# A decoder-layer kernel on one Trainium2 core: two additions moved into accumulating DMAs, level masks left out, conv taps of one instruction each, and another load order in the FFN's second product

## The chip, the cores and the metric

The kernel runs on one core of a Trainium2 chip, in one launch. The metric is the device time of that launch in microseconds (us), lower is better. A core has five engines that run their own instruction streams in order and wait for each other by semaphores: PE (matmuls; its weight loads are counted as PEld), DVE, ACT, POOL and SP. DMAs are issued from the queues of SP and of POOL and move data by 16 shared DMA engines.

## What is computed

One step of a hybrid decoder layer on 1024 prompt tokens and 8 x 8 sample tokens, width 1024, all in float32. Cut to what matters here:

```python
def swiglu(x, w_in, w_out):
    gate, up = jnp.split(x @ w_in, 2, axis=-1)
    return (jax.nn.silu(gate) * up) @ w_out

x = x + 0.5 * swiglu(rmsnorm(x), w_ffn1_in, w_ffn1_out)          # D_FF = 2816
qkv_raw, z, a, b, q_s, k_s, v_s, gate_a, gate_b = split(rmsnorm(x) @ w_in)
ext = concat([conv_buf, qkv_raw])                                # 4 taps
q, k, v = split(silu(sum(conv_w[j] * ext[:, j:j + L] for j in range(4))))
# gated delta rule, 8 heads of 128:
decay = exp(where(incl, gc[..., :, None] - gc[..., None, :], -inf))
A = where(strict, (k * beta) @ k.T * decay, 0)
T = triangular_solve(A + eye, eye)
...
o_g = rmsnorm(o_g) * silu(z)
o_s = windowed attention with sinks (q_s, k_s, v_s)
mixed = sigmoid(gate_a) * o_g + sigmoid(gate_b) * o_s
x = x + mixed @ w_out
x = x + 0.5 * swiglu(rmsnorm(x), w_ffn2_in, w_ffn2_out)
y = rmsnorm(x)
```

## The kernel before

All matmuls are done on a float32 value split into a high and a low part (`split`, L225 on ACT casts the high part, L226 on DVE subtracts it to get the low part); a product is three matmuls (L250 to L252, in the second product of the FFN L713 to L715). 1088 columns of tokens (1024 and 64) lie beside each other; in the GDN they are nine chunks of 128.

The stages in order: the first FFN (its first product, then the second, `ffn_out`, from about 528 us), the attention, the GDN (`gdn`, about 1150 to 1950 us, in which the dense products of all heads are woven between the recurrences of others), the out projection and the second FFN (`ffn2`; its `ffn_out` starts at about 2525 us).

**FFN-out.** It works in seven products j with five groups of weight tiles each. `rights` (L602 on) loads the rows of h from DRAM (hq, hd) into two buffers h0 and h1 in turn, and splits each into x0 to x3. `lefts` loads the weights into w0, w1, tq (as w2 and v) and w3, in halves k = 0 and 1, splits them into u0 to u3, and has POOL and DVE form the sums of halves (L653 to L660). For j = 0 only the halves k = 0 are needed. Loads go out on SP's queue in the order in which they are written (`keep_in_program_order`); a load waits on the queue until its buffer is free, and holds what stands behind it. `rights` issues the load of step i + 2 behind the split of step i; `lefts` issues in j = 0, from the second group on, the next group's half 0 and the previous group's half 1.

**Conv taps** (`conv_taps`). The input ext holds 1024 prompt columns and then eight blocks of 11 sample columns. Four taps per q, k and v of a head: the first on ACT (L1205, L1206), three on DVE (L1208 on 1024 columns, L1209 on 8 x 8), then silu on ACT (L1210).

**Decay** (`decay`). SP loads a broadcast of the head's cumulated gates into dm (128 x 1152, 576 KB; L1330), ACT applies nine Relus (L1333, one per chunk) and an Exp (L1334), POOL multiplies by two masks (L1335, L1336). `stage_t` then uses dm on DVE (L1367, L1462).

**Levels** (`levels`). The triangular inverse is put together in two block levels from A (the tile am0). For each, POOL masks a part of A into `am` (L1410, L1437), PE multiplies it with the inverse so far (L1416, L1440), ACT copies the results out (x2z L1421, t4 L1433, x3z L1441), and PE multiplies again (L1426, L1445). Each head has three such groups of chunks.

**Gated output** (`gdn_out`). The attention has written its gated part to the DRAM tensor me. Behind each of three parts of a head's gated output zg, POOL loads me (L1652) and adds it (L1653), then stores zg to md (L1655). `ffn2` loads md into its tiles a.

The order on each engine comes from a planner at build time, which sees data dependencies and its own estimates; it is the same in each run. POOL's and SP's instructions and DMAs are executed in order too.

Of the kernel before, what the change touches and what calls it, by code (L numbers as in the profile page):

```python
# [18 lines left out]
P = 128  # L19
# [33 lines left out]
def constants():  # L53
# [17 lines left out]
        "m2": (j // 64 == i // 64) & (j % 64 < 32) & (i % 64 >= 32),  # L71
        "m3": (j < 64) & (i >= 64),
# [4 lines left out]
        "new": np.where(new, 0.0, NEG),  # L77
    }
# [77 lines left out]
class Core:  # L156
# [34 lines left out]
    def setup(self):  # L191
# [12 lines left out]
        self.md = self.dp.tile([H, P, T], F32, name="md")  # L204
# [402 lines left out]
    def rights(self):  # L607
# [11 lines left out]
        for i, (n, _) in enumerate(src):  # L619
            z = fo[f"h{i % 2}"].rearrange("p (n t) -> p n t", n=2)[:, :n]  # L620
            out = self.split_to(f"x{i % 4}", z, i < 2)
            load(i + 2)
            yield out

    def lefts(self, w_out):
# [13 lines left out]
        load(0, 0)  # L639
        for j in range(7):  # L640
            for i in range(len(GROUPS)):
                a11, a21, a12, a22 = quads(i)
                if j == 0 and i:
                    if i == 1:
                        load(1, 0)
                    load(i + 1, 0)
                    load(i - 1, 1)
                if j == 1 and i == 0:
                    load(len(GROUPS) - 1, 1)
# [544 lines left out]
    def conv_taps(self, h, d, u):  # L1194
        nc, v = self.nc, self.nc.vector
        self.lab = f"h{h}"
        blk, u_ = u * 8 + h, "qkv"[u]
        y, ext = d[u_], d["ext", u]
        es = ext[:, 1027:1115].rearrange("p (b j) -> p b j", j=11)
        v.memset(y[:, T:], 0.0)  # L1200
        ys = y[:, LP:T].rearrange("p (b t) -> p b t", t=NT)
        for j in range(4):
            wc = self.cw[:, j * 24 + blk:j * 24 + blk + 1]
            if j == 0:
                nc.scalar.mul(y[:, :LP], ext[:, 0:LP], wc)  # L1205
                nc.scalar.mul(ys, es[:, :, 0:NT], wc)  # L1206
            else:
                v.scalar_tensor_tensor(out=y[:, :LP], in0=ext[:, j:j + LP], scalar=wc, in1=y[:, :LP], op0=ALU.mult, op1=ALU.add)  # L1208
                v.scalar_tensor_tensor(out=ys, in0=es[:, :, j:j + NT], scalar=wc, in1=ys, op0=ALU.mult, op1=ALU.add)  # L1209
        nc.scalar.activation(y[:, :T], y[:, :T], AF.Silu)  # L1210
# [14 lines left out]
    def gdn(self):  # L1225
        nc, v = self.nc, self.nc.vector
        with ExitStack() as st:
            gp = self.pool("gdn", stack=st)
            a, n = self.off["m2"]
            self.m2 = gp.tile([P, 2, 32], F32, name="m2")  # L1230
            nc.sync.dma_start(self.m2, self.i["c_pack"][:, a:a + n].rearrange("p (b u j) -> p b u j", b=2, u=2)[:, :, 1, :])
            a, n = self.off["m3"]
            self.m3 = gp.tile([P, 64], F32, name="m3")
            nc.sync.dma_start(self.m3, self.i["c_pack"][:, a + 64:a + n])
# [12 lines left out]
            bp = Pools(self, st, ("L", "X", "pr", "am"), ("S0", "kg", "vt", "qk"), ("t4",), ("R", "o1", "vn", "S", "jk", "*"), ("ot", "zg", "me", "s4"), ("e",), ("y",), ("dm", "am0"))  # L1247
# [78 lines left out]
    def decay(self, bp, h, d):  # L1326
# [4 lines left out]
                          self.rw[h * NCH:(h + 1) * NCH, :].rearrange("(o c) t -> o (c t)", o=1).broadcast_to([P, TP]))  # L1331
        for c in range(NCH):
            nc.scalar.activation(dm[:, c], dm[:, c], AF.Relu, scale=-1.0, bias=self.gc[:, h, c:c + 1])  # L1333
        nc.scalar.activation(dm, dm, AF.Exp, scale=-1.0)  # L1334
        nc.gpsimd.tensor_tensor(out=dm[:, 0:8], in0=dm[:, 0:8], in1=self.tri[:, None, :].broadcast_to([P, 8, P]), op=ALU.mult)  # L1335
        nc.gpsimd.tensor_tensor(out=dm[:, 8], in0=dm[:, 8], in1=self.tris, op=ALU.mult)  # L1336
# [69 lines left out]
    def levels(self, bp, h, A, t4):  # L1406
        nc, v = self.nc, self.nc.vector
        self.lab = f"h{h}"
        am = bp.tile([P, 4, 2, 32], F32, tag="am", bufs=2, name=self.name("am"))
        nc.gpsimd.tensor_tensor(out=am, in0=A.rearrange("p c (b u j) -> p c b u j", b=2, u=2)[:, :, :, 1, :],  # L1410
                                in1=self.m2[:, None].broadcast_to([P, 4, 2, 32]), op=ALU.mult)
# [530 lines left out]
```

## Time and profile before

| | us |
|---|---|
| median of 3 runs (2808.99 to 2811.06) | 2810.89 |
| profiled execution | 2810.84 |
| its span | 2809.1 |
| PE busy | 2691.2 |
| DVE busy | 1982.4 |
| ACT busy | 1237.3 |
| POOL busy | 563.7 |

Mean granted clock of PE 0.983. The chain of work that ended last is PE in 77% of the span, DVE 9%, DMA 5%, ACT 3%, issue 3% and POOL 1%. The profile is of one execution; its time is that of the median run. "Waits" rows give an engine's idle time by the instruction that stood waiting and the one that released it; in a timeline the brackets hold the idle time just ahead of the instruction and its releaser. The granted clock is a share of full speed, 1.00 and 0.50 being the two levels of 2.4 and 1.2 GHz.

### The profile page before, as it was taken

The numbers are of one execution on the slowest core, as the hardware profiler recorded it, in microseconds if no ns is written. First come the engines' busy times: TensorE is split into PE (matmuls) and PEld (weight loads), VectorE is DVE, ScalarE is ACT, GpSimd is POOL, SyncE is SP. The second block draws the span as 40 slices with busy tenths as digits, with TensorE's granted clock in tenths as the row PEclk, the third lists the DMA queues.
The fourth block names the chain that finished last, engine by engine and source line by source line (L and its number), as shares of the span: only waits on it lengthen the run. The fifth ranks groups of instructions, "written<-read, shape, count | busy, mean of one in ns | idle before, by whom it ended". The sixth has DMA issues, their size and how long they took to land.

```text
span 2809.1 us, 50868 instructions
## 1 busy us (share of the span) xinstructions
PE 2691.2 (96%) x19887; PEld 2523.4 (90%) x19887; DVE 1982.4 (71%) x4502; ACT 1237.3 (44%) x2904; POOL 563.7 (20%) x585
## 2 busy tenths in 40 slices
PE   6999999999989999999999999999999999998998
PEld 6899999999978888887788888888989999997998
DVE  6777787564665777777887776785678878767545
ACT  5333322233334767753655455546444233223333
POOL 3222221231010000031332222221002212205110
PEclk9999999999999999999999999999999999999999
DMA  4243322546332333342333333334533322216562
GB/s 143 91 158 127 112 101 90 191 135 144 107 105 54 85 85 78 97 100 63 90 98 78 67 94 90 89 82 145 191 118 117 103 88 102 100 57 237 129 147 78
DMA packets 236871, 306.66 MB, mean 109 GB/s; under 512 B 14405, under 2 KB 184214, under 8 KB 236598
## 3 DMA queue, kind: packets, MB, share of 16 engines
q1 hardware_dynamic: 203252, 222.21, 25.9%
q0 software_dynamic: 33312, 81.19, 10.6%
q8 instruction: 156, 2.56, 0.4%
q14 instruction: 85, 0.70, 0.1%
q10 hardware_dynamic: 66, 0.02, 0.0%
HBM read 212.19 MB, written 84.19 MB: 106 GB/s over the span
## 4 chain that ended last, share of the span: by engine, by line
PE 77%; DVE 9%; DMA 5%; ACT 3%; issue 3%; POOL 1%; SPq 0%; DVEq 0%; ACTq 0%; POOLq 0%
PE pst L252 13%; PE pst L250 13%; PE pst L251 13%; PE pst L715 4%; PE pst L714 4%; PE pst L713 4%; PE psgh L250 3%; PE psgh L251 3%; PE psgh L252 3%; PE psg L250 3%; PE psg L252 3%; PE psg L251 3%; PE pso L943 1%; DMA adr<-am0h 1%; PE pst L936 1%
## 5 line engine op out<-in xcount | busy, mean ns | idle before, releaser
L251 PE MATMUL pst<-x,u 128*128 128x256 f32 (+3 forms) x2656 | 780.4, 294 | 1.0 <-DVE x L226 1.0
L250 PE MATMUL pst<-x,u 128*128 128x256 f32 (+3 forms) x2040 | 610.8, 300 | 12.1 <-ACT x L225 11.1
L252 PE MATMUL pst<-x,u 128*128 128x256 f32 (+3 forms) x2040 | 605.6, 297 | 0.0
L251 PEld LDWEIGHTS pst<-x,u 128*128 128x128 f32 x2656 | 503.8, 190 | 7.1 <-DVE x L226 1.5
L250 PEld LDWEIGHTS pst<-x,u 128*128 128x128 f32 x2040 | 386.3, 190 | 19.3 <-ACT x L225 12.6
L252 PEld LDWEIGHTS pst<-x,u 128*128 128x128 f32 x2040 | 387.4, 190 | 4.6
L225 ACT CAST u<-raw 128x512 fp32r<-128x512 f32 x308 | 186.4, 617 | 323.3 <-PE pst L252 300.6
L715 PE MATMUL pst<-x,u 128*128 128x272 f32 x1008 | 293.3, 292 | 13.8 <-DVE u L226 13.8
L252 PE MATMUL psgh<-xhl,wlh 128*128 128x512 f32 (+2 forms) x912 | 303.7, 333 | 0.0
L713 PE MATMUL pst<-x,u 128*128 128x272 f32 x1008 | 290.6, 292 | 7.4 <-ACT x L225 7.1
L714 PE MATMUL pst<-x,u 128*128 128x272 f32 x1008 | 293.2, 292 | 4.5 <-DVE x L226 4.5
L226 DVE TENSOR_TENSOR u<-raw,u 128x512 fp32r<-128x512 f32 x308 | 216.5, 712 | 49.6 <-ACT u L225 49.3
L334 DVE TENSOR_TENSOR tm<-pst,tm 128x256 f32<-128x256 f32 (+1 forms) x400 | 168.0, 434 | 103.0 <-PE pst L252 100.9
L252 PE MATMUL pst<-xhl,u 128*128 128x256 f32 (+2 forms) x808 | 237.8, 295 | 2.5 <-DVE u L226 2.5
L250 PE MATMUL pst<-xhl,u 128*128 128x256 f32 (+2 forms) x808 | 236.7, 294 | 2.2 <-ACT u L225 2.2
L715 PEld LDWEIGHTS pst<-x,u 128*128 128x128 f32 x1008 | 192.8, 191 | 14.6 <-DVE u L226 14.6
L713 PEld LDWEIGHTS pst<-x,u 128*128 128x128 f32 x1008 | 191.6, 192 | 8.3 <-ACT x L225 7.5
L714 PEld LDWEIGHTS pst<-x,u 128*128 128x128 f32 x1008 | 192.9, 191 | 4.9 <-DVE x L226 4.9
L252 PEld LDWEIGHTS psgh<-xhl,wlh 128*128 128x128 f32 x912 | 172.9, 190 | 12.2
L252 PEld LDWEIGHTS pst<-xhl,u 128*128 128x128 f32 x808 | 153.2, 190 | 5.9 <-DVE u L226 2.9
L250 PEld LDWEIGHTS pst<-xhl,u 128*128 128x128 f32 x808 | 152.8, 190 | 5.3 <-ACT u L225 2.4
L250 PE MATMUL psg<-xhl,whc 128*128 128x512 f32 (+2 forms) x456 | 153.3, 336 | 1.1 <-DVE ring L814 1.1
(686 smaller groups left out, 6356.3 us busy)
## 6 DMA issues: line engine op xcount, KB each, us to landing
raw<-in_w_ffn_in_dram SPq DMA_DIRECT2D x48, 1024.0 KB
h<-hq SPq DMA_DIRECT2D x56, 544.0 KB
hq<-sg POOLq DMA_DIRECT2D x45, 544.0 KB, 3.6
rawh<-in_w_in_dram SPq DMA_DIRECT2D x38, 512.0 KB
w<-in_w_ffn_out_dram SPq DMA_DIRECT2D x14, 1024.0 KB
raw<-in_w_in_dram SPq DMA_DIRECT2D x21, 512.0 KB
ring<-ring SPq DMA_DIRECT2D x32, 272.0 KB
t4h<-tdr POOLq DMA_DIRECT2D x32, 256.0 KB, 5.1
```

The costliest lines, as they stand in the source:

```text
L225: keep(self.nc.scalar.copy(hi, src))
L226: return keep(self.nc.vector.tensor_tensor(out=lo, in0=src, in1=hi.bitcast(F32), op=ALU.subtract))
L250: nc.tensor.matmul(out, w[0], x[0], start=start, stop=False)
L251: nc.tensor.matmul(out, w[0], x[1], start=False, stop=False)
L252: nc.tensor.matmul(out, w[1], x[0], start=False, stop=stop)
L334: v.tensor_tensor(out=out, in0=pb, in1=t[:, i, :n], op=ALU.add)
L713: nc.tensor.matmul(pb, w[0], y[0], start=first, stop=False, skip_group_check=True)
L714: nc.tensor.matmul(pb, w[0], y[1], start=False, stop=False, skip_group_check=True)
L715: nc.tensor.matmul(pb, w[1], y[0], start=False, stop=end, skip_group_check=True)
L936: nc.tensor.transpose(out=pt[:, kb, r], in_=sm[:, r, kb * P:(kb + 1) * P], identity=self.ident)
L943: nc.tensor.matmul(po, w[:, ks // P + kb].rearrange("p a b -> p (a b)"), x[:, kb].rearrange("p r q -> p (r q)"), start=i + kb == 0, stop=i ...
```

## The change

- `decay`: a constant `later` (0 where the mask was 1, NEG elsewhere, 128 x 1152) is added to dm by an accumulating DMA on POOL's queue, behind the broadcast and ahead of the Relus. The two mask multiplies are gone.
- `levels`: the masks m2 and m3, the tile `am` and the two mask multiplies of each group are gone; PE reads A itself.
- `conv_taps`: each tap is one instruction on 1112 columns that runs over the prompt and the sample blocks alike; silu is two instructions, and the memset stands behind it.
- `gdn_out`: zg is added to me in DRAM by one accumulating DMA; the loads of me, POOL's adds and the store to md are gone, and `ffn2` reads me.
- `rights`: the load of step i + 1 is issued ahead of the split of step i, from the second step on. `lefts`: a table says at which step which half is loaded; the halves k = 1 come a group later, and w1 and w2 ahead of the third h load.

```diff
--- before.py
+++ after.py
@@ -68,13 +68,12 @@
         "suf": j > i,
         "sufs": same8 & (j > i),
         "m1": (j // 32 == i // 32) & (j % 32 < 16) & (i % 32 >= 16),
-        "m2": (j // 64 == i // 64) & (j % 64 < 32) & (i % 64 >= 32),
-        "m3": (j < 64) & (i >= 64),
         "bm": (np.arange(P)[:, None] // 8 == np.arange(NB)[None, :]),
         "band": np.where(band, 0.0, NEG),
         "first": np.where(first, 0.0, NEG),
         "cache": np.where(cache, 0.0, NEG),
         "new": np.where(new, 0.0, NEG),
+        "later": np.concatenate([np.where(j <= i, 0.0, NEG)] * 8 + [np.where(same8 & (j <= i), 0.0, NEG)], axis=1),
     }
     off, parts, at = {}, [], 0
     for k, v in mats.items():
@@ -201,7 +200,6 @@
         self.hq = self.dp.tile([7, NS // 2, P, HT], F32, name="hq")
         self.xt = self.dp.tile([P, KD, T], F32, name="xt")
         self.xd = self.dp.tile([P, KD, T], F32, name="xd")
-        self.md = self.dp.tile([H, P, T], F32, name="md")
         self.me = self.dp.tile([H, P, T], F32, name="me")
         self.cols = self.cp.tile([P, 33], F32, name="cols")
 
@@ -617,10 +615,10 @@
         load(0)
         load(1)
         for i, (n, _) in enumerate(src):
+            if i:
+                load(i + 1)
             z = fo[f"h{i % 2}"].rearrange("p (n t) -> p n t", n=2)[:, :n]
-            out = self.split_to(f"x{i % 4}", z, i < 2)
-            load(i + 2)
-            yield out
+            yield self.split_to(f"x{i % 4}", z, i < 2)
 
     def lefts(self, w_out):
 
@@ -636,17 +634,12 @@
             return [ws[i][:, :, k, 512 * h:512 * h + 512] for k in range(2) for h in range(2)]
 
         at = 0
-        load(0, 0)
+        order = {(0, 0): ((0, 0),), (0, 1): ((1, 0), (2, 0)), (0, 2): ((3, 0), (0, 1)), (0, 3): ((4, 0), (1, 1)), (0, 4): ((2, 1), (3, 1)), (1, 0): ((4, 1),)}
         for j in range(7):
             for i in range(len(GROUPS)):
                 a11, a21, a12, a22 = quads(i)
-                if j == 0 and i:
-                    if i == 1:
-                        load(1, 0)
-                    load(i + 1, 0)
-                    load(i - 1, 1)
-                if j == 1 and i == 0:
-                    load(len(GROUPS) - 1, 1)
+                for z in order.get((j, i), ()):
+                    load(*z)
                 if j == 2:
                     n = GROUPS[i][1]
                     s = fo[f"S{i % 2}"].rearrange("p (n c) -> p n c", c=512)[:, :n]
@@ -1196,18 +1189,16 @@
         self.lab = f"h{h}"
         blk, u_ = u * 8 + h, "qkv"[u]
         y, ext = d[u_], d["ext", u]
-        es = ext[:, 1027:1115].rearrange("p (b j) -> p b j", j=11)
-        v.memset(y[:, T:], 0.0)
-        ys = y[:, LP:T].rearrange("p (b t) -> p b t", t=NT)
+        n = 1112
         for j in range(4):
             wc = self.cw[:, j * 24 + blk:j * 24 + blk + 1]
             if j == 0:
-                nc.scalar.mul(y[:, :LP], ext[:, 0:LP], wc)
-                nc.scalar.mul(ys, es[:, :, 0:NT], wc)
+                nc.scalar.mul(y[:, :n], ext[:, 0:n], wc)
             else:
-                v.scalar_tensor_tensor(out=y[:, :LP], in0=ext[:, j:j + LP], scalar=wc, in1=y[:, :LP], op0=ALU.mult, op1=ALU.add)
-                v.scalar_tensor_tensor(out=ys, in0=es[:, :, j:j + NT], scalar=wc, in1=ys, op0=ALU.mult, op1=ALU.add)
-        nc.scalar.activation(y[:, :T], y[:, :T], AF.Silu)
+                v.scalar_tensor_tensor(out=y[:, :n], in0=ext[:, j:j + n], scalar=wc, in1=y[:, :n], op0=ALU.mult, op1=ALU.add)
+        nc.scalar.activation(y[:, :LP], y[:, :LP], AF.Silu)
+        nc.scalar.activation(y[:, LP:T].rearrange("p (b t) -> p b t", t=NT), y[:, 1027:1115].rearrange("p (b j) -> p b j", j=11)[:, :, :NT], AF.Silu)
+        v.memset(y[:, T:], 0.0)
 
     def tail_out(self, bp, h, tails):
         nc = self.nc
@@ -1226,12 +1217,6 @@
         nc, v = self.nc, self.nc.vector
         with ExitStack() as st:
             gp = self.pool("gdn", stack=st)
-            a, n = self.off["m2"]
-            self.m2 = gp.tile([P, 2, 32], F32, name="m2")
-            nc.sync.dma_start(self.m2, self.i["c_pack"][:, a:a + n].rearrange("p (b u j) -> p b u j", b=2, u=2)[:, :, 1, :])
-            a, n = self.off["m3"]
-            self.m3 = gp.tile([P, 64], F32, name="m3")
-            nc.sync.dma_start(self.m3, self.i["c_pack"][:, a + 64:a + n])
             self.gn = self.cols[:, 32:33]
             self.x2z = gp.tile([P, 4, 2, 32], F32, name="x2z")
             self.x3z = gp.tile([P, 4, 64], F32, name="x3z")
@@ -1244,7 +1229,7 @@
             for u in range(2):
                 for z in range(2):
                     nc.gpsimd.dma_start(self.rows_view(self.td[u], z), self.rsm[:, None, :].broadcast_to([P, NCH, P]))
-            bp = Pools(self, st, ("L", "X", "pr", "am"), ("S0", "kg", "vt", "qk"), ("t4",), ("R", "o1", "vn", "S", "jk", "*"), ("ot", "zg", "me", "s4"), ("e",), ("y",), ("dm", "am0"))
+            bp = Pools(self, st, ("L", "X", "pr"), ("S0", "kg", "vt", "qk"), ("t4",), ("R", "o1", "vn", "S", "jk", "*"), ("ot", "zg", "s4"), ("e",), ("y",), ("dm", "am0"))
             hd = [dict() for _ in range(H)]
             wv = Weave(self)
 
@@ -1329,11 +1314,11 @@
         dm = d["dm"] = bp.tile([P, NCH, P], F32, tag="dm", bufs=2, name=self.name("dm"))
         nc.sync.dma_start(dm.rearrange("p c t -> p (c t)"),
                           self.rw[h * NCH:(h + 1) * NCH, :].rearrange("(o c) t -> o (c t)", o=1).broadcast_to([P, TP]))
+        a, n = self.off["later"]
+        nc.gpsimd.dma_start(dm.rearrange("p c t -> p (c t)"), self.i["c_pack"][:, a:a + n], accum_op=ALU.add)
         for c in range(NCH):
             nc.scalar.activation(dm[:, c], dm[:, c], AF.Relu, scale=-1.0, bias=self.gc[:, h, c:c + 1])
         nc.scalar.activation(dm, dm, AF.Exp, scale=-1.0)
-        nc.gpsimd.tensor_tensor(out=dm[:, 0:8], in0=dm[:, 0:8], in1=self.tri[:, None, :].broadcast_to([P, 8, P]), op=ALU.mult)
-        nc.gpsimd.tensor_tensor(out=dm[:, 8], in0=dm[:, 8], in1=self.tris, op=ALU.mult)
 
     def stage_t(self, bp, h, d, prev):
         self.lab = f"h{h}"
@@ -1406,14 +1391,11 @@
     def levels(self, bp, h, A, t4):
         nc, v = self.nc, self.nc.vector
         self.lab = f"h{h}"
-        am = bp.tile([P, 4, 2, 32], F32, tag="am", bufs=2, name=self.name("am"))
-        nc.gpsimd.tensor_tensor(out=am, in0=A.rearrange("p c (b u j) -> p c b u j", b=2, u=2)[:, :, :, 1, :],
-                                in1=self.m2[:, None].broadcast_to([P, 4, 2, 32]), op=ALU.mult)
         px = self.bank("o").rearrange("p (w c b j) -> p w c b j", w=2, c=4, b=2)
         for c in range(4):
             for b in range(2):
                 lo, hi = b * 64, b * 64 + 32
-                nc.tensor.matmul(px[hi:hi + 32, 0, c, b], am[:, c, b], t4[:, c, 0, lo:hi], start=True, stop=True, tile_position=(0, hi))
+                nc.tensor.matmul(px[hi:hi + 32, 0, c, b], A[:, c, hi:hi + 32], t4[:, c, 0, lo:hi], start=True, stop=True, tile_position=(0, hi))
         yield .5, LHOP
         self.lab = f"h{h}"
         for b in range(2):
@@ -1433,11 +1415,9 @@
             nc.scalar.copy(t4[lo:hi, :, 1, hi:hi + 32], px[lo:hi, 1, :, b])
         yield 0, LHOP
         self.lab = f"h{h}"
-        am = bp.tile([P, 4, 64], F32, tag="am", bufs=2, name=self.name("am"))
-        nc.gpsimd.tensor_tensor(out=am, in0=A[:, :, 64:], in1=self.m3[:, None, :].broadcast_to([P, 4, 64]), op=ALU.mult)
         px = self.bank("o").rearrange("p (w c j) -> p w c j", w=2, c=4)
         for c in range(4):
-            nc.tensor.matmul(px[64:, 0, c], am[:, c], t4[:, c, 0, 0:64], start=True, stop=True, tile_position=(0, 64))
+            nc.tensor.matmul(px[64:, 0, c], A[:, c, 64:], t4[:, c, 0, 0:64], start=True, stop=True, tile_position=(0, 64))
         nc.scalar.copy(self.x3z[64:], px[64:, 0])
         yield .45, LHOP
         self.lab = f"h{h}"
@@ -1646,13 +1626,8 @@
                 v.scalar_tensor_tensor(out=zg[:, cs], in0=pb[:, :n], scalar=self.gn, in1=zg[:, cs], op0=ALU.mult, op1=ALU.mult)
                 yield m * .11, 1.0
                 self.lab = f"h{h}"
-                if last:
-                    continue
-                me = bp.tile([P, 512], F32, tag="me", bufs=1, name=self.name("me"))
-                nc.gpsimd.dma_start(me[:, :n], self.me[h][:, cs])
-                nc.gpsimd.tensor_tensor(out=zg[:, cs], in0=zg[:, cs], in1=me[:, :n], op=ALU.add)
         if not last:
-            nc.gpsimd.dma_start(self.md[h], zg)
+            nc.gpsimd.dma_start(self.me[h], zg, accum_op=ALU.add)
 
     def ffn2(self):
         nc, v = self.nc, self.nc.vector
@@ -1670,7 +1645,7 @@
             aq.tile([P, 1408], F32, name="gap")
             a = {h: (aq if h in (4, 5) else ap).tile([P, T], F32, tag="al" if h in (2, 3, 6) else "ah", bufs=2, name=self.name("a")) for h in (2, 3, 0, 1, 4, 5, 6)}
             for h in range(H - 1):
-                nc.sync.dma_start(a[h], self.md[h])
+                nc.sync.dma_start(a[h], self.me[h])
                 if h == 3:
                     ws = list(self.units_direct(self.pair_raw(wo, 0)))
             for k in range(0, KD, 2):
```

**SP's queue at the start of the first FFN-out.** w0, w1, w3 and tq (w2) are the weight tiles, h0 and h1 the two buffers of h. Before:

```order
L633 DMA w0_677_5811<-in_w_ffn1_out_dram 128x2x1024
L615 DMA h0_675_5809<-hq_67 128x2x544
L615 DMA h1_676_5810<-hq_67 128x2x544
L615 DMA h0_675_5809<-hq_67 128x2x544
L633 DMA w1_678_5812<-in_w_ffn1_out_dram 128x2x1024
L633 DMA tq_663_5795<-in_w_ffn1_out_dram 128x2x1024
L633 DMA w0_677_5811<-in_w_ffn1_out_dram 128x2x1024
L615 DMA h1_676_5810<-hq_67 128x2x544
L615 DMA h0_675_5809<-hq_67 128x544
```

With the change:

```order
L631 DMA w0_677_5810<-in_w_ffn1_out_dram 128x2x1024
L613 DMA h0_675_5808<-hq_67 128x2x544
L613 DMA h1_676_5809<-hq_67 128x2x544
L631 DMA w1_678_5811<-in_w_ffn1_out_dram 128x2x1024
L631 DMA tq_663_5794<-in_w_ffn1_out_dram 128x2x1024
L613 DMA h0_675_5808<-hq_67 128x2x544
L613 DMA h1_676_5809<-hq_67 128x2x544
L631 DMA w3_679_5812<-in_w_ffn1_out_dram 128x2x1024
L631 DMA w0_677_5810<-in_w_ffn1_out_dram 128x2x1024
```

w1 and tq have moved ahead of the second load into h0, and w3 ahead of the second half of w0.

**DVE there, behind the splits of the first weight and h tiles (u0, x0).** x and u are the split tiles, S0 and S1 sums of halves. Before (the row behind these is the split u0 of tq, 128 x 512):

```order
L226 TENSOR_TENSOR x2_667_5799<-h0_675_5809,x2_667_5799 128x1088
L226 TENSOR_TENSOR u1_673_5805<-w1_678_5812,u1_673_5805 128x1024
L226 TENSOR_TENSOR x1_672_5804<-h1_676_5810,x1_672_5804 128x1088
L226 TENSOR_TENSOR u2_668_5800<-tq_663_5795,u2_668_5800 128x1024
L653 TENSOR_TENSOR S0_664_5796<-w0_677_5811 128x1024
L226 TENSOR_TENSOR x3_669_5801<-h1_676_5810,x3_669_5801 128x1088
L226 TENSOR_TENSOR x0_665_5797<-h0_675_5809,x0_665_5797 128x544
L226 TENSOR_TENSOR u1_673_5805<-w0_677_5811,u1_673_5805 128x1024
L226 TENSOR_TENSOR u3_670_5802<-w3_679_5813,u3_670_5802 128x1024
L653 TENSOR_TENSOR S1_680_5814<-w1_678_5812 128x1024
L226 TENSOR_TENSOR u2_668_5800<-w1_678_5812,u2_668_5800 128x1024
L226 TENSOR_TENSOR x1_672_5804<-h1_676_5810,x1_672_5804 128x1088
```

With the change:

```order
L224 TENSOR_TENSOR u1_673_5804<-w1_678_5811,u1_673_5804 128x1024
L224 TENSOR_TENSOR x1_672_5803<-h1_676_5809,x1_672_5803 128x1088
L224 TENSOR_TENSOR u2_668_5799<-tq_663_5794,u2_668_5799 128x1024
L224 TENSOR_TENSOR x2_667_5798<-h0_675_5808,x2_667_5798 128x1088
L224 TENSOR_TENSOR x3_669_5800<-h1_676_5809,x3_669_5800 128x1088
L224 TENSOR_TENSOR u3_670_5801<-w3_679_5812,u3_670_5801 128x1024
L646 TENSOR_TENSOR S0_664_5795<-w0_677_5810 128x1024
L224 TENSOR_TENSOR u1_673_5804<-w0_677_5810,u1_673_5804 128x1024
L224 TENSOR_TENSOR x0_665_5796<-h0_675_5808,x0_665_5796 128x544
L224 TENSOR_TENSOR u0_666_5797<-tq_663_5794,u0_666_5797 128x512
L646 TENSOR_TENSOR S1_680_5813<-w1_678_5811 128x1024
L224 TENSOR_TENSOR u2_668_5799<-w1_678_5811,u2_668_5799 128x1024
```

x2 has moved behind u1, x1 and u2, the split u3 ahead of S0, and the split u0 of tq (128 x 512) from behind all of these to the tenth row; in both lists 15 instructions of this kind, u0 and x0 included, stand ahead of the first evictions.

**ACT in the GDN, at the decay of head 4.** dm is the decay tile; t4 and x3z belong to the levels of a head ahead of it, y to the conv, zg to the gate. Before, from the first Relu on dm:

```order
L1333 ACTIVATE dmh_2115_16861<-dmh_2115_16861,gc 128x128
L1433 COPY t4h_2068_16570<-psoh_2100_16720 32x4x32
L1333 ACTIVATE dmh_2115_16861<-dmh_2115_16861,gc 128x128 x2
L1433 COPY t4h_2068_16570<-psoh_2100_16720 32x4x32
L1210 ACTIVATE yh_2114_16850<-yh_2114_16850 128x1088
L1473 ACTIVATE jkh_2109_16799,sqh_1980_16193<-oth_1979_16192 128x128
L1596 ACTIVATE zgh_2087_16672<-psgh_2106_16758 128x256
L1441 COPY x3z<-psoh_2112_16824 64x256
L1333 ACTIVATE dmh_2115_16861<-dmh_2115_16861,gc 128x128 x6
L1334 ACT_TABLE_LOAD
L1334 ACTIVATE dmh_2115_16861<-dmh_2115_16861 128x1152
L1596 ACT_TABLE_LOAD
```

With the change:

```order
L1415 COPY t4h_2050_16486<-psoh_2081_16634 32x4x32
L1200 ACTIVATE yh_2094_16762<-yh_2094_16762 128x64
L1576 ACTIVATE zgh_2069_16588<-psgh_2087_16672 128x256
L1415 COPY t4h_2050_16486<-psoh_2081_16634 32x4x32
L1453 ACTIVATE jkh_2090_16713,sqh_1962_16109<-oth_1961_16108 128x128
L1421 COPY x3z<-psoh_2092_16736 64x256
L1320 ACTIVATE dmh_2095_16770<-dmh_2095_16770,gc 128x128 x6
L1576 ACTIVATE zgh_2069_16588<-psgh_2091_16729 128x320
L1320 ACTIVATE dmh_2095_16770<-dmh_2095_16770,gc 128x128 x3
L1199 ACTIVATE yh_2093_16761<-yh_2093_16761 128x1024
L1321 ACT_TABLE_LOAD
L1321 ACTIVATE dmh_2095_16770<-dmh_2095_16770 128x1152
```

The Relus have moved behind the copies t4 and x3z and the silu of k. POOL's accumulating DMA into this dm stands behind the loads of t4 and two memsets and ahead of the copies kqs.

## Rows read from the trace of the kernel before

**Rows 1.** The page: busy us (share of the span) and instructions of each engine.

```profile
PE 2691.2 (96%) x19887; PEld 2523.4 (90%) x19887; DVE 1982.4 (71%) x4502; ACT 1237.3 (44%) x2904; POOL 563.7 (20%) x585
```

**Rows 2.** Windows: us, busy us (instructions) of each engine, granted clock, DMA share, GB/s.

```profile
500.00:600.00 100.00, 88.03 (x653) 86.95 (x652) 66.38 (x67) 31.60 (x42) 40.27 (x15) 0.93 0.50 179
1150.00:1950.00 800.00, 761.01 (x5787) 667.49 (x5786) 575.70 (x1841) 431.11 (x1268) 193.05 (x243) 0.98 0.35 89
```

**Rows 3.** Waits of PE, 515 to 606: us in total, times, longest.

```profile
PE pst L715 <- DVE u L226: 6.8, 2, 6.5
PE pst L713 <- ACT x L225: 2.7, 1, 2.7
```

**Rows 4.** Waits of PE, 2500 to 2606.

```profile
PE pst L715 <- DVE u L226: 7.0, 2, 6.5
PE pst L713 <- ACT x L225: 4.3, 1, 4.3
```

**Rows 5.** Timeline of SP's queue, from 517: start, us, instructions.

```profile
517.63 14.40 SPq L615 DMA_DIRECT2D h<-hq  x3
532.27 0.92 SPq L633 DMA_DIRECT2D w<-in_w_ffn_out_dram  x1
```

**Rows 6.** Windows, ahead of and in the first wait, columns as in rows 2.

```profile
526.00:530.00 4.00, 3.22 (x23) 2.79 (x21) 2.87 (x6) 0.00 (x0) 0.39 (x1) 1.00 0.00 2
538.00:540.00 2.00, 0.88 (x8) 0.66 (x6) 1.29 (x1) 0.63 (x2) 0.00 (x0) 1.00 1.03 420
```

**Rows 7.** Timeline of DVE, splits of x in the first FFN-out.

```profile
538.16 1.29 DVE L226 TENSOR_TENSOR x<-h,x 128x1088 fp32r<-128x1088 f32 x1 [6.51 <-ACT x L225]
...
562.57 3.42 DVE L226 TENSOR_TENSOR x<-h,x 128x1088 fp32r<-128x1088 f32 x1
```

**Rows 8.** Timeline of POOL beside the second of these.

```profile
561.52 3.32 POOL L660 TENSOR_TENSOR w<-w 128x1024 f32<-128x1024 f32 x1
```

**Rows 9.** The taps by line: ns min/median/max, first and last start.

```profile
L1208 DVE SCALAR_TENSOR_TENSOR yh<-exth,cw,yh x72: 1205/1272/1716, 1185.3 to 1893.9; 128x1024 f32<-128x1024 f32 x72
...
L1209 DVE SCALAR_TENSOR_TENSOR yh<-exth,cw,yh x72: 265/274/1407, 1186.5 to 1895.4; 128x64 f32<-128x64 f32 x72
```

**Rows 10.** DMA issues of POOL: count, KB each, median us to landing.

```profile
md<-zgh POOLq DMA_DIRECT2D x7, 544.0 KB, 3.3
...
acc<-xt POOLq DMA_DIRECT2D x4, 512.0 KB, 6.8
...
acc<-xt POOLq DMA_DIRECT2D x4, 320.0 KB, 12.9
```

**Rows 11.** Waits of PE in the GDN, 1150 to 1950.

```profile
PE psth L1456 <- DVE qkh L1462: 4.7, 4, 1.7
PE psth L1456 <- DVE zgh L1646: 4.0, 2, 2.5
PE psgh L1351 <- ACT yh L1210: 3.1, 3, 1.7
```

**Rows 12.** Timeline of SP's queue: dm's load, heads 4 and 7.

```profile
1525.92 0.45 SPq L1330 DMA_DIRECT2D dmh<-rw  x1
...
1805.53 0.45 SPq L1330 DMA_DIRECT2D dmh<-rw  x1
```

**Rows 13.** Timeline of ACT from dm's landing to the x2z copy, head 4's dm.

```profile
1529.73 0.40 ACT L1333 ACTIVATE dmh<-dmh,gc 128x128 f32<-128x128 f32 x1 [3.34 <-DMA dmh<-rw]
...
1533.41 1.87 ACT L1333 ACTIVATE dmh<-dmh,gc 128x128 f32<-128x128 f32 x6
...
1541.46 0.53 ACT L1421 COPY x2z<-psoh 32x128 f32<-32x128 f32 x2
```

**Rows 14.** Timeline of PE: level products, heads 4 and 7's dm.

```profile
1531.21 0.68 PE L1440 MATMUL psoh<-t4h,amh 128*64 128x64 f32 x8 [1.61 <-ACT t4h L1433]
...
1542.35 0.22 PE L1426 MATMUL psoh<-x2z,t4h 128*32 128x32 f32 x1
...
1821.73 0.22 PE L1426 MATMUL psoh<-x2z,t4h 128*32 128x32 f32 x1 [1.33 <-ACT x2z L1421]
```

## The prediction

> **What bounds it.** I read the engines' busy shares first: PE is busy 96% of the span [rows 1]. So time is won or lost only where PE stands still, and I looked for those places by windows, then asked the waits of PE who ends them. Two kinds of place touch this change. In the 100 us around the start of the first FFN's second product PE is idle 12.0 us and its granted clock averages 0.93; in the 800 us of the GDN it is idle 39.0 us at 0.98 [rows 2]. In both, clock is lost beside the idle time: 7% of 100 us and 2% of 800 us. Part of that low clock lies in the idle time itself, so I charge 0.2 us of clock for each us of idle, half of what the GDN row would give (16 / 39).
>
> **FFN-out loads.** The waits around the first FFN-out are 6.5 us for one DVE split of a weight tile and 2.7 us for ACT's first cast of h [rows 3]; the second FFN-out shows the same pair, 6.5 and 4.3 [rows 4]. Their source is on SP's queue: three h loads are issued from 517.63, the third waits for the first h buffer, so the queue stands for 14.4 us and the second w load goes out only at 532.27 [rows 5]. While the queue stands, the DMA engines are idle (share 0.00 in 526 to 530); when it opens they are saturated (1.03, 420 GB/s, in 538 to 540) and PE runs dry [rows 6]. In the order of the change w1 and w2 stand ahead of the third h load, and their buffers are long free, so 2 MB move into the idle stretch. The first wait (2.7) should go. The second falls behind a queue of DVE splits which starts at 538.16 [rows 7]. It would start near 532.0, where the first x split ends and the old queue opens [rows 5], some 6 us sooner, and in the new order the split that PE waited for is the twelfth of the fifteen, no longer the last. PE takes the groups in the order in which they are split, so 6 us of lead and three places in the order are set against 6.5 us of wait, and I count it as gone. Per FFN-out 2.7 + 6.5 and 4.3 + 6.5: 20 us idle, 24 with clock. Against that: DVE splits take 3.42 us beside a POOL operation of 3.32 us but 1.29 alone [rows 7, 8], and this work remains. I leave 3 us for it: **-21 us**. The Trainium skill ("SBUF — State Buffer", Who interferes with whom) says that VectorE and GpSimd share a port pair as an exclusive lock; the rows agree (a split as long as the POOL operation beside it). By that rule alone the two engines' work adds up whatever the loads do, which is the second rival below.
>
> **Taps, gate and level masks.** Each tap loses its 64-column instruction (72 of 0.27 us, 19.7 us) and widens the other by 1112/1024 (72 x 1.27 x 0.086 = 7.9 us) [rows 9]: DVE gets 12 us shorter. POOL loses all multiplies by masks and the adds of the two branches, with their loads of me; POOL isn't on PE's path here, but each such operation can hold a DVE one as above. One accumulating DMA per head takes the place of loads, adds and store, and frees zg sooner; its consumer is the FFN2 stage, far off, so I cost it at nothing. If that cover is gone it would cost one DMA's landing at FFN2's start, under 13 us even by the slowest row [rows 10]. PE's waits in the GDN on DVE's qk, zg and on the conv's silu are 4.7, 4.0 and 3.1 us [rows 11], 11.8 together. All three are behind DVE's queue; bounds 0 and 11.8. I take two thirds, as DVE is shortened in every head: 8 us, with clock **-9.6 us**. Fewer table loads and the one silu more on ACT cancel within a few us on an engine busy 44%; ACT's position in the chain is costed next.
>
> **Decay by an accumulating DMA.** This part adds a wait. Before: SP issues dm's broadcast at 1525.92, the first Relu starts at 1529.73, so 3.8 us [rows 12, 13]. POOL's two mask multiplies came after the Exp and far ahead of dm's reader, so removing them frees nothing on the path. Now a second transfer of 576 KB, issued by POOL after the first has landed, stands between, and ACT, which works in order, stops at the Relu until it lands. Queued behind the Relus on ACT are a zg eviction, q's silu, two table loads, the Exp, a weight cast and the x2z copy for which PE waits. Before: from the six Relus at 1533.41 to the end of the x2z copy (1541.46 + 0.53) is 8.6 us [rows 13]; three Relus at 0.31 and a 0.35 us silu more make 9.9 us. The nearest accumulating DMA is acc<-xt, 512 KB in 6.8 us; those of 320 KB queued behind it take 12.9, and the plain store of 544 KB takes 3.3 [rows 10]. I take 6.7: same kind, alone in its queue, and somewhat less scattered. So x2z is ready 3.8 + 6.7 + 9.9 = 20.4 us after SP's issue. PE reached its reader at 1542.35 after a 1.61 us stop at L1440 that came from the same dm wait [rows 14]; the new order puts L1440's copies ahead of the Relu. Thus PE is there 14.8 us after the issue and stops for 5.6 us. Head 7: 1805.53 to 1821.73 with 1.33 of stop in it, 14.9, stops 5.5 [rows 12, 14]. The same pair in heads 5 and 6 lies 17.1 and 17.4 us apart (four heads in all): 3.3 and 3.0. Sum 17.4, with clock 20.9; the two old stops go (2.9, with clock 3.5): **+17.4 us**. Heads 0 to 3 load dm where ACT has less queued behind it; bounds 0 and 9 (half a later head's in each), I take **+3 us**.
>
> The Trainium skill ("DMA: Bandwidth & Descriptors", Anatomy of one DMA) fits a GpSimd-issued DMA as 2.0 us + bytes/436e3, which gives an estimate of 3.4 us for these 590 KB. The acc<-xt row is twice its 3.2 for 512 KB, so the row decides. "Collectives: The Full Stack" (Why ReduceScatter is half of AllGather) says that a DMA that adds reads two sources; that speaks against this change and would lift the estimate to 4.7, still under the row.
>
> **Sum.** -21 - 9.6 + 17.4 + 3 = -10.2 on the profiled 2810.84 us, which is the median of the runs shown to 0.1 us: **2801 us**. No change from the old time within 0.2% (what a measurement of this kernel can tell) means 2805.2 to 2816.5.
>
> **Rivals.**
> - *The accumulating DMA is cheap* (3.3 us, like the plain store [rows 10]). For it: it has long rows and the queue to itself. Against: acc<-xt. x2z comes 3.4 us sooner, stops fall to 2.2, 0, 0 and 2.1; 4.3, with clock 5.2, less 3.5, and 1 for the early heads: -21 - 9.6 + 2.7 = -28, so 2783. Chance 0.20.
> - *DVE and POOL remain the bound of the FFN-out*: only the first waits (2.7 and 4.3, with clock 8.4) go, the 6.5 us waits stay, as the slow splits [rows 7, 8] are no shorter. 2801 + 12.6 is about 2814. Against: the order moves the awaited split forward. Chance 0.15.
> - *The accumulating DMA is slow, and the kernel ends slower*: 12.9 us, as the queued ones [rows 10], because weights and states load beside it and the DMA waits its turn. Each of four heads stops 6.2 us longer: 24.8, with clock 30, so 2831. It decides from where the DMA takes over 9.9 us (3.2 us more in four heads, with clock 15.5). Against: acc<-xt is slow only behind its own kind. Chance 0.20.
> The forecast has 0.45.
>
> **Chances.** The forecast's own spread, mostly the 8 us of taps and the 3 us of early heads, is 2792 to 2811, so its 0.45 gives 0.29 faster, 0.14 the same, 0.02 slower. The cheap DMA gives 0.20 faster; the bound FFN-out 0.10 the same and 0.05 slower; the slow DMA 0.16 slower and 0.04 the same. Faster 0.49, same 0.28, slower 0.23. The range runs from the cheap DMA's time, 2782, into the slow one's, 2824, where the DMA takes 11.5 us; what it leaves out is the rest of the slow case and of unnamed ones.
>
> **What would show it.** In the profile after: the second w load issued near 518.5, no DMA share of zero in 526 to 530, and PE's waits in both FFN-outs down to the first DVE split and a few us; the two rows of 2.7 and 4.3 gone if the loads were the cause, the 6.5 us rows still there if the port is. In the GDN: a row "ACT dmh <- DMA" well above 18.3 us, now ended by the accumulating DMA, and new waits of PE on x2z of 3 to 6 us in heads 4 to 7; the DMA's own row says which rival holds (3, 7 or 13 us). Taps of about 1.38 us, no 64-column ones, and smaller waits of PE for qk and zg. The prediction is wrong in its core if PE has no x2z stops of over 2 us in the GDN, or if the FFN-outs' idle stays at 12 us.

## The result, and the profile after

The change is slower: 2832.73 us (median of 4 runs, 2831.92 to 2835.25) against 2809.94 for the kernel before, a ratio of 1.0085 with a 95% interval of 1.0069 to 1.0101. The forecast of 2801 us had the wrong sign, and the time lies above the range (2782 to 2824).

Windows of the changed kernel, columns as in [rows 2]: the first FFN-out, the sample attention with the first conv products, and the rest of the GDN.

```profile
500.00:600.00 100.00, 90.98 (x692) 89.92 (x691) 74.86 (x71) 33.70 (x45) 46.27 (x19) 0.97 0.54 185
1150.00:1250.00 100.00, 70.46 (x558) 61.67 (x557) 55.39 (x271) 47.43 (x143) 14.53 (x32) 0.88 0.41 103
1250.00:1950.00 700.00, 661.63 (x4998) 583.96 (x4996) 484.25 (x1451) 360.13 (x1062) 92.29 (x120) 0.97 0.36 81
```

The last two stretches in the kernel before:

```profile
1150.00:1250.00 100.00, 94.76 (x730) 83.05 (x729) 70.90 (x305) 62.99 (x167) 21.16 (x39) 1.00 0.43 114
1250.00:1950.00 700.00, 666.26 (x5059) 584.45 (x5058) 504.80 (x1537) 368.12 (x1101) 171.88 (x204) 0.98 0.34 85
```

The idle time of PE fell from 12.0 us [rows 2] to 9.0 in the first FFN-out, and grew from 33.7 to 38.4 in the GDN behind 1250. But the big number stands at the sample attention, of which the prediction didn't speak: in 1150 to 1250 idle went from 5.2 us to 29.5 and the granted clock from 1.00 to 0.88. PE's waits in the stretch of [rows 11] say for what:

```profile
PE pst L988 <- DMA kcache<-in_cache_swa_k_dram: 16.7, 1, 16.7
PE psgh L1336 <- ACT tgh L1585: 12.8, 4, 5.1
PE psoh L1408 <- ACT x2z L1403: 9.2, 2, 5.5
PE pso L1026 <- DVE os L1032: 7.7, 7, 1.7
...
PE psth L1436 <- DVE zgh L1626: 0.8, 2, 0.5
...
PE psgh L1336 <- ACT yh L1199: 0.6, 1, 0.6
```

One wait of 16.7 us for the load of kcache (the key cache of the sample attention) was not there before, and the waits for DVE between the steps of that attention (the row of os) grew from 0.9 us to 7.7. The waits for qk, zg and silu of [rows 11] are nearly gone (zg from 4.0 to 0.8, silu from 3.1 to 0.6, qk in no row of the answer); in their place stand ACT's tg and x2z. PE around the big wait, and SP's issue of the load:

```profile
1177.36 0.50 PE L936 MATMUL pso<-tl,vh 128*128 128x256 f32 x2
1194.58 1.75 PE L988 MATMUL pst<-ident,kcache 128*128 128x128 f32 x7 [16.72 <-DMA kcache<-in_cache_swa_k_dram]
```

```profile
1180.90 0.43 SPq L976 DMA_DIRECT2D kcache<-in_cache_swa_k_dram  x1
```

The same two in the kernel before:

```profile
1196.06 1.03 PE L995 MATMUL pst<-ident,kcache 128*128 128x128 f32 x8
```

```profile
1187.37 0.45 SPq L983 DMA_DIRECT2D kcache<-in_cache_swa_k_dram  x1
```

The load is issued at 1180.90, 6.5 us earlier than before (1187.37), and was never in PE's way there. What changed is what PE has to do meanwhile. The order of the built program, PE, from the last product of the prompt attention (pso <- tl) on, cut to one row per block; psgh are the dense products of head 0's conv. Before:

```
MATMUL pso<-tl,vh 128x256
MATMUL psgh<-xhl,whc 128x512, 24 rows
MATMUL psgh<-xhl,whc 128x256, 24 rows
MATMUL psgh<-xhl,whc 128x320, 8 rows and more
MATMUL pst<-ident,kcache 128x128
```

With the change:

```
MATMUL pso<-tl,vh 128x256
MATMUL pst<-ident,kcache 128x128
...
MATMUL pso<-ptS,vcd 128x128 (the last of the sample attention)
MATMUL psgh<-xhl,whc 128x512, 24 rows
```

The dense products that covered the load, and later filled the gaps of the sample attention, stand behind it now. The reason is in the addresses of the built program. The first conv output tile of head 0, `ext`, lies at bytes 103392 to 108000 of each partition before, and at 98784 to 103392 after: 4608 bytes lower, which is the size of the tiles that the change freed ahead of it (m2 and m3 256 each, am and me 2048 each). The sample attention's tile ptS ends at 99456. So `ext` now overlaps a tile that is in use until the sample attention ends, and in the built program ACT's first write to it waits for that attention's last product. Before, it waited for nothing.

The other places: the two FFN-outs, PE's waits [rows 3, 4]:

```profile
PE pst L706 <- DVE acc L683: 4.1, 1, 4.1
PE pst L707 <- DVE x L224: 4.1, 2, 2.4
PE pst L708 <- DVE u L224: 0.7, 1, 0.7
```

```profile
PE pst L706 <- DVE acc L683: 4.2, 1, 4.2
PE pst L707 <- DVE x L224: 2.1, 1, 2.1
```

The first waits (2.7 and 4.3) are gone, and in the place of the second (6.5) there are 4.1 and 4.2, now at the start of the second product. (The DVE x rows hold the split ahead of the first matmul, 2.4 and 2.1 us, which stood there before too; the other 1.7 us in the first FFN-out are new.) ACT's wait for dm, DMA issues and taps:

```profile
ACT dmh L1320 <- DMA dmh<-in_c_pack_dram: 45.2, 7, 14.9
```

```profile
dmh<-in_c_pack_dram POOLq DMA_DIRECT2D x8, 576.0 KB, 6.6
...
me<-zgh POOLq DMA_DIRECT2D x7, 544.0 KB, 5.8
```

```profile
L1198 DVE SCALAR_TENSOR_TENSOR yh<-exth,cw,yh x72: 1306/1368/1378, 1236.5 to 1922.7; 128x1112 f32<-128x1112 f32 x72
```

The accumulating DMA takes 6.6 us (forecast 6.7), ACT's waits for dm grew from 18.3 us to 45.2, and a tap of 1112 columns takes 1.37 us (forecast 1.38).

### The profile page after: what moved, and what is told of

Same layout as the page of the kernel before. It is cut to its first block, busy times and chain, and to the rows that moved or that the text cites. A ratio compares the mean times of both kernels' runs of the same rounds, so it can differ in the third digit from the quotient of the medians.

```text
span 2830.1 us, 50708 instructions
## 1 busy us (share of the span) xinstructions
PE 2694.0 (95%) x19887; PEld 2529.8 (89%) x19887; DVE 1967.8 (70%) x4430; ACT 1230.8 (43%) x2900; POOL 484.6 (17%) x503
```

## The experiments

Two theories came first. **M**: the freed memory moved `ext` onto the sample attention, and that costs most of it. **D**: the decay's DMA, by holding ACT, is behind the sample attention's stall too. All ratios are to runs of the kernel before on the same chip.

**An unused tile in place of the freed ones.**

```diff
             gp = self.pool("gdn", stack=st)
+            gp.tile([P, 1152], F32, name="gap")
```

> The changed kernel with one unused tile of 4608 bytes per partition at the start of the GDN's pool, so that the tiles behind it lie where they lay in the kernel before. Theory M (the freed tiles m2, m3, am and me moved head 0's first conv tile onto memory that the sample attention still uses, so the planner put 13 us of dense matmuls behind it): about 27 us less than the change, 2806 us, and PE's wait for kcache (16.7 us) gone. Theory D (the decay's accumulating DMA, by holding ACT at the first Relus, makes that stall too): within 3 us of the change, 2832, the kcache wait still there.

Measured 2809.12 us, ratio 1.0003 (0.9993 to 1.0013): the time of the kernel before, 23 us below the change. M holds for that; D falls as the whole cause. PE's waits:

```profile
PE psgh L1337 <- ACT tgh L1586: 12.2, 3, 4.5
PE psoh L1409 <- ACT x2z L1404: 11.0, 2, 5.7
PE pst L988 <- DMA kcache<-in_cache_swa_k_dram: 6.3, 1, 6.3
```

A kcache wait of 6.3 us is left, which M did not foresee: the load is issued at 1184.83 and PE goes on at 1199.07, 14.2 us later, where in the kernel before PE found it landed 8.7 us after the issue (1187.37 to 1196.06).

**The same shift in the kernel before.**

```diff
-("L", "X", "pr", "am"), ... ("ot", "zg", "me", "s4"), ("e",), ("y",), ("dm", "am0"))
+("L", "X", "pr"), ... ("ot", "zg", "s4"), ("e",), ("y",), ("dm", "am0"), ("am", "me"))
```

> The kernel before, with nothing but the pools of the tiles am and me moved behind all others, so that the conv tiles lie 4096 bytes lower. Theory M: about 27 us slower than the kernel before, 2837, with a kcache wait of some 16 us. Theory D: no change, 2810.

Measured 2826.84, ratio 1.0070 (1.0054 to 1.0085), 20 us slower with not one instruction changed:

```profile
PE pst L995 <- DMA kcache<-in_cache_swa_k_dram: 10.7, 1, 10.7
PE pso L1033 <- DVE os L1039: 7.7, 7, 1.7
```

The kcache wait is 10.7 us here, and the 7.7 us of waits within the attention are those of the change. What is missing to the change's 16.7 is the 6 us left above, and the load itself shows it: here, without an accumulating DMA, it was issued at 1186.89 and PE went on at 1194.44, 7.6 us later; in the change it took 13.7 us, with the unused tile 14.2.

**Multiplies in place of the accumulating DMA** (on the kernel with the unused tile).

```diff
-        nc.gpsimd.dma_start(dm..., self.i["c_pack"][:, a:a + n], accum_op=ALU.add)
...
+        nc.gpsimd.tensor_tensor(out=dm[:, 0:8], in0=dm[:, 0:8], in1=self.tri..., op=ALU.mult)
+        nc.gpsimd.tensor_tensor(out=dm[:, 8], in0=dm[:, 8], in1=self.tris, op=ALU.mult)
```

> The changed kernel with the unused tile, and the decay's mask by POOL's two multiplies again instead of the accumulating DMA. By the trace the GDN lost about 9 us in sum, of which the taps should have won up to 10, so the decay's DMA costs 15 to 20: M expects 2806 - 17 = 2789 and ACT's waits for dm back near 18 us. If the DMA cost nothing that is on the path, the time stays at the one of the kernel with the unused tile, 2806. D expects 2790 as well; it differs in the run with the unused tile alone.

Measured 2783.96, ratio 0.9917 (0.9902 to 0.9931), so it beats both kernels, by 23 us and 47. The DMA costs 1.0003 - 0.9917 of 2807 us, 24 us, more than expected. ACT's waits for dm are down to:

```profile
ACT dmh L1319 <- DMA dmh<-rw: 8.9, 5, 2.5
```

**The load order alone** (`rights` and `lefts` of the change on the kernel before).

> The kernel before with the new load order of the FFN's second product alone. By the offsets of the two traces: 10 us less, 2800, with two waits of PE of about 4 us for DVE's evictions left. By the prediction's term: 21 us less, 2789. By the rival that DVE and POOL stay the bound: 8 us less, 2802.

Measured 2798.09, ratio 0.9967 (0.9955 to 0.9979), 9 us. PE's waits, and the DVE rows that end the first:

```profile
PE pst L708 <- DVE acc L685: 4.1, 1, 4.1
PE pst L709 <- DVE x L226: 4.1, 2, 2.4
```

```profile
558.90 3.43 DVE L226 TENSOR_TENSOR x<-h,x 128x1088 fp32r<-128x1088 f32 x1
562.26 1.12 DVE L685 TENSOR_SCALAR acc<-pst 128x272 f32<-128x272 f32 x3
```

The split of x at 558.90 is the slow kind, and the evictions stand behind it.

**All evictions of the first product on ACT.**

```diff
-                if (i + c) % 2:
+                if j == 0 or (i + c) % 2:
```

> The kernel with the unused tile and mask multiplies, with all evictions of the FFN-out's first product on ACT, which stands idle there, in the place of half on DVE behind the last split. If PE's 4.1 us waits at the start of the second product are for the banks that DVE evicts late: 8 us less, 2776. If they are for the split of x that ends at the same time: within 2 us, 2784.

Measured 2786.09, ratio 0.9916 (0.9901 to 0.9930), the same as without. The wait changes its name from acc to x, as the split ends when the evictions began:

```profile
PE pst L707 <- DVE x L224: 8.2, 3, 3.6
```

**POOL's sums left out** (on the load order alone).

```diff
-                    g.tensor_tensor(out=a12, in0=a12, in1=s, op=ALU.subtract)
...
-                    g.tensor_tensor(out=a11, in0=a11, in1=a21, op=ALU.subtract)
...
-                    g.tensor_tensor(out=a21, in0=a21, in1=a22, op=ALU.add)
```

> The kernel before with the new load order, and POOL's sums of weight halves left out in both FFN-outs (the second product then multiplies the wrong halves; this is part of the computation). If DVE's splits are late because they take turns with POOL's sums (3.4 us in the place of 1.3): no split over 1.4 us, the two waits of 4 us gone, 8 to 10 us less than with the load order alone, 2789. If the splits are late because the loads are: no change, 2798.

Measured 2780.56, ratio 0.9894 (0.9878 to 0.9911), 18 us below the load order alone by the medians and 20 by the ratios, twice what was expected. The same split, and all that PE waits for in the first FFN-out:

```profile
552.23 1.29 DVE L226 TENSOR_TENSOR x<-h,x 128x1088 fp32r<-128x1088 f32 x1
```

```profile
PE pst L704 <- DVE x L226: 2.4, 1, 2.4
```

1.29 us in the place of 3.43, and the 4 us wait is gone. In 530 to 600 and 2480 to 2600 together, PE's idle time is 24.9 us before, 14.1 with the load order and 2.9 without the sums. So the order of the loads was one part of the idle time, and the turns that DVE and POOL take another of the same size. The granted clock in 530 to 600 rose with it, from 0.96 to 1.00 (the upper level); where the rest of the gain lies was not traced.

**The decay's DMA alone**, on the kernel before with all tiles kept.

> The kernel before with the decay's accumulating DMA alone (mask multiplies gone, all tiles of the pools kept). Theory W (the DMA's landing time, 6.6 us, stands in front of ACT's Relus and so in front of what PE waits for): as much slower as the kernel with the multiplies put back was faster, some 22 to 25 us, 2832, with ACT's waits for dm up by 20 us or more, among them some 6 us at the sample attention, whose kcache load shares the DMA engines with it. Rival P (the loss came only together with the other order of the taps): under 10 us slower, 2817.

Measured 2824.21, ratio 1.0050 (1.0032 to 1.0069): 14 us, between the two. ACT waits as expected, and the kcache wait is there without any freed tile:

```profile
ACT dmh L1336 <- DMA dmh<-in_c_pack_dram: 37.4, 7, 7.5
```

```profile
PE pst L996 <- DMA kcache<-in_cache_swa_k_dram: 7.1, 1, 7.1
PE psoh L1427 <- ACT x2z L1422: 6.6, 2, 3.8
PE psgh L1352 <- ACT tgh L1606: 6.5, 3, 2.6
```

**The first two heads with multiplies, the others by DMA** (unused tile in).

```diff
+        if h > 1:
             nc.gpsimd.dma_start(dm..., accum_op=ALU.add)
...
+        if h < 2:
+            nc.gpsimd.tensor_tensor(...)
```

> The changed kernel with the unused tile, where heads 0 and 1 have their decay masked by multiplies and only heads 2 to 7 by the accumulating DMA. Theory C (the first two accumulating DMAs delay the kcache load at the sample attention, for which PE waits 6.3 us): that wait gone, 7 us less than with all heads, 2802. If the wait is there without them: 2809.

Measured 2802.20, ratio 0.9981 (0.9972 to 0.9990), 6 us below all heads by DMA, and no kcache row is left among PE's waits: PE finds it landed 8.2 us after the issue (1183.18 to 1191.39). Theory C holds: these two DMAs, issued just after the kcache load, hold up its landing. The other 18 of the 24 us are in heads 2 to 7.

**The DMA twice.**

```diff
         nc.gpsimd.dma_start(dm..., accum_op=ALU.add)
+        nc.gpsimd.dma_start(dm..., accum_op=ALU.add)
```

> The changed kernel with the unused tile, and the accumulating DMA issued twice for each dm. Theory W (its landing time stands in front of the Relus): ACT waits some 6 us more per head, the same price as the first one, 20 to 28 us slower, 2833. If the first DMA costs by its place in the order alone, and the planner moves the Relus behind both: under 8 us slower, 2816.

Measured 2831.43, ratio 1.0078 (1.0063 to 1.0093), 21 us above once. ACT's and PE's waits, against 34.3, 12.2 and 11.0 with one:

```profile
ACT dmh L1322 <- DMA dmh<-in_c_pack_dram: 55.0, 8, 11.6
```

```profile
PE psgh L1338 <- ACT tgh L1587: 17.0, 4, 7.8
PE psoh L1410 <- ACT x2z L1405: 13.6, 2, 8.9
```

The price of the second is about that of the first, as theory W has it. A second DMA also doubles the traffic, which this run can't tell apart from the landing time. Against the traffic speak the names of the grown waits, ACT's tg and x2z and no load, and the share of the DMA engines in 1250 to 1950: 0.36 with the multiplies, 0.38 with one DMA and 0.40 with two.

**dm loaded a head earlier, with a third buffer.**

```diff
-        tag="dm", bufs=2
+        tag="dm", bufs=3     (broadcast and accumulating DMA in decay_load)
...
                     k_done(h + 2)
+                    if h + 3 < H:
+                        self.decay_load(bp, h + 3, hd[h + 3])
```

> The changed kernel with a third dm buffer and dm's broadcast and accumulating DMA issued one head earlier, and 720 bytes of unused tile. Theory W: ACT's waits for dm fall from 34 us (with the unused tile alone) to under 8 and the time to that with mask multiplies, 2784, give or take 5 for the sample attention, where the first three dm transfers now stand together. If what the DMA costs is its traffic on the DMA engines and not its place ahead of the Relus: no gain, 2809.

Measured 2799.61, ratio 0.9969 (0.9957 to 0.9980), 10 us of the 24. It decides little between the two: the planner moved the Relus forward together with the loads, and ACT waits as long as with two buffers. PE's waits for x2z fell from 11.0 us to 0.9, but its wait for kcache doubled from 6.3 us:

```profile
ACT dmh L1331 <- DMA dmh<-in_c_pack_dram: 32.8, 5, 11.2
```

```profile
PE pst L988 <- DMA kcache<-in_cache_swa_k_dram: 12.9, 1, 12.9
PE psgh L1347 <- ACT tgh L1596: 10.7, 4, 3.4
```

**The taps alone, and levels and gate alone.**

> The kernel before with the one-instruction taps alone. DVE loses 14.5 us of busy time in the GDN. By the prediction's term (two thirds of the waits for qk, zg and silu, with clock): 9.6 us less, 2798. If DVE's time isn't what PE waits for, no change, 2808. From the difference between the run with mask multiplies and that with the loads alone, 14 us for taps, levels and gate together, I expect 5 to 10 of it here.

> The kernel before with the level masks left out and the gated output added by an accumulating DMA, and an unused tile of 4608 bytes in the place of the freed ones. By the prediction nothing of its own beyond a shorter hold of DVE: 0 to 3 us less, 2806. If it is the rest of the 14 us that the loads don't explain: 5 to 9 us less, 2800.

Measured 2804.35, ratio 0.9983 (0.9974 to 0.9992), and 2800.56, ratio 0.9971 (0.9961 to 0.9981): 5 us for the taps, 8 for the part that was costed at nothing.

## Why the prediction was wrong

- **The step that failed is a missing one**: that freeing am, me, m2 and m3 costs and moves nothing. The prediction followed instructions on SP, DVE, ACT and POOL and never asked what lies in the place of a freed tile. That is 23 us, shown from both sides: the unused tile takes them away, and the shift alone (4096 of the 4608 bytes) costs the kernel before 20. The change ended 24 us slower where 10 us faster were forecast. Of these 34 us, 23 are this step, 11.7 the FFN-out loads and 3.7 the decay; the taps and the rest gave 3.3 more than forecast, which leaves 1 us over. With the unused tile the change takes 2809 us, inside the range, but still without the 10 us of gain.
- **FFN-out loads, -21 us forecast, 9 measured.** The mechanism of the first waits [rows 3 to 6] was right: both are gone. The step "6 us of lead and three places in the order are set against 6.5 us of wait, and I count it as gone" failed. The split that PE waited for did end 12 us sooner (556.77 in the place of 568.73), but behind it stand splits of 3.4 us beside POOL's sums, and 4 us came back as a wait at the start of the second product. That "their buffers are long free" held for w1 (issued at 517.71) and not for w2, whose load waited for PE until 527.08. The cause is that of the second rival, and its sum is close (8.4 us of gain left, 9 measured), but not its rows: it had the 6.5 us waits stay, and these went. The 3 us left for it were too few.
- **Taps and the rest, -9.6 forecast, 5 + 8 measured.** The sum came near by luck, its parts were off: the 12 us that DVE gains were worth half of the term, and "costed at nothing" for levels and gate was wrong. Through which wait POOL's multiplies and adds had cost those 8 us was not tried apart.
- **Decay, +17.4 and +3 forecast, 24 measured in this kernel.** The price of the DMA (6.7 against 6.6 to 7.0 us) and the chain behind the Relus were right. The stops of PE for x2z and tg with the unused tile, heads 3 to 7:

```profile
1449.73 4.21 PE L1337 MATMUL psgh<-yh 128*128 128x128 f32 x18 [3.44 <-ACT tgh L1586]
...
1549.64 0.26 PE L1409 MATMUL psoh<-x2z,t4h 128*32 128x32 f32 x1 [5.26 <-ACT x2z L1404]
...
1644.32 2.07 PE L1337 MATMUL psgh<-yh 128*128 128x128 f32 x8 [4.34 <-ACT tgh L1586]
...
1739.37 1.86 PE L1337 MATMUL psgh<-yh 128*128 128x128 f32 x7 [4.46 <-ACT tgh L1586]
...
1835.49 0.26 PE L1409 MATMUL psoh<-x2z,t4h 128*32 128x32 f32 x1 [5.74 <-ACT x2z L1404]
```

  In heads 4 to 7 5.3, 4.3, 4.5 and 5.7, sum 19.8 where 17.4 were forecast (5.6, 3.3, 3.0, 5.5). Two of them came at tg, an eviction that stands just ahead of x2z on ACT:

```profile
1643.68 0.59 ACT L1586 ACTIVATE tgh<-psgh 128x512 f32<-128x512 f32 x1
1644.29 0.53 ACT L1404 COPY x2z<-psoh 32x128 f32<-32x128 f32 x2
```

  The early heads were the weak spot, 3 us forecast: head 3 stops for 3.4 us in the same way, and where dm and kcache meet on the DMA engines it is 6 us at one place. These stops are more than the 24 us; other waits became shorter (the silu row, 7.8 us with the multiplies, is 0.6 with the DMA).
- **Chances.** The slow rival (2831 us, 0.20) had the right sign and nearly the time, but by luck: it rests on a DMA of 12.9 us, which took 6.6.

Measured alone on the kernel before, the gains are 9, 5 and 8 us and the decay's DMA costs 14; with the 23 us that the unused tile took off the change, the sum is 15 us slower, where the whole is 24 slower (0.85% of 2807). The 9 us between are about what the decay's DMA costs more beside the other parts (24) than alone (14). In the first case PE's x2z and tg waits are 6.6 and 6.5 us, in the second 11.0 and 12.2, at about the same wait of ACT. Why PE is nearer to ACT there was not tried; that stays open.

## What to carry to other kernels

Freeing a tile is a change of addresses: before costing it at nothing, look at which tile slides into the place, who used that memory last, and whether the first writer now waits for it; an unused tile of the same size tells in one run. A DMA put between a load and an engine that works in order holds everything queued behind for its landing time (6.6 to 7.0 us here, of which PE's stops were 3.4 to 5.7), even where its own result isn't needed for long: with the unused tile, DVE read dm 11 and 12 us behind the Exp in heads 5 and 4. Where DVE and POOL work side by side, add their times before counting on an earlier start.

## What the runs showed of the hardware that was not expected

Two accumulating DMAs of 576 KB, issued up to 5 us behind a plain load of 1 MB on another queue, held that load's landing up by 6 to 7 us: 13.7 to 14.4 us from issue in the five runs where PE waited for it beside them, 7.6 in the one where it waited without them. And leaving out POOL's sums shortened DVE's splits from 3.4 to 1.3 us and the kernel by 18 us (20 by the ratios), though POOL is busy for only 20% of the span. The Trainium skill's rule of the exclusive port pair ("SBUF — State Buffer", Who interferes with whom) agrees with the splits. Waits for the sums' results, which went with them, show in no row: with the load order alone, neither PE nor DVE nor ACT has a wait for POOL in 526 to 720 or 2480 to 2770. An accumulating DMA into DRAM (me, 544 KB) took 5.8 us where the plain store of the same size took 3.3 [rows 10].
